# One hybrid decoder layer on one core: a kept block of zeros, a transposing swish, reordered FFN rounds and a paired last quarter

## The chip, the cores and the metric

The kernel runs on one core of a Trainium2 chip. Such a core has a matrix engine (TensorE, PE in the profile), a vector engine (VectorE, DVE), an activation engine (ScalarE, ACT), a general engine (GpSimd, POOL), an engine that issues transfers (SyncE, SP), an on-chip memory of 128 partitions (SBUF) and an accumulator memory for the matrix engine's results (PSUM). Each engine takes its instructions in its own fixed order and waits on semaphores for the others. The metric is device microseconds per execution; lower is better.

## The reference

One layer on 1024 tokens of width 1024, in fp32. `rmsnorm` and `layernorm` are the usual ones, and the six rows of `mod` come from the vector `c`.

```python
h = rmsnorm(x, pre_mix_g) * (1.0 + sc1) + sh1
glu_in, qkv, gates = split(h @ w_in)
u = u_val * sigmoid(u_gate)                        # 512 channels
u = causal_depthwise_conv(u, conv_w, conv_b)       # 31 taps
u = silu(layernorm(u, conv_ln_g, conv_ln_b))
y_conv = u @ w_conv_out
o = stick_breaking_attention(q, k, v)              # 8 heads of 64, strictly causal
y_att = o @ w_att_out
merged = sigmoid(g_conv) * y_conv + sigmoid(g_att) * y_att
x = x + ga1 * rmsnorm(merged @ w_o, post_mix_g)
h = rmsnorm(x, pre_ffn_g) * (1.0 + sc2) + sh2
gate, up = split(h @ w_ffn_in)                     # d_ff = 2816
x = x + ga2 * rmsnorm((silu(gate) * up) @ w_ffn_out, post_ffn_g)
```

In the attention a query's weights come from `sigmoid(z)` and a running product over the keys before it, so a 128-token block above the diagonal is zero.

## The kernel before

**Tiling.** Activations lie with channels on the partitions and tokens along the free axis, in two halves of 512 tokens. A product of fp32 matrices is made of three: each operand is split into a rounded part (`_hi`, made by ACT as a copy) and a remainder (`_lo`, made by VectorE as a subtraction), and PE multiplies hi·hi, lo·hi and hi·lo into one PSUM bank. A "product" below means 12 matmuls of 128 x 512, four row blocks by three.

**Stages**, with their place in the profiled execution: start, norm and `mod` (to 60 us); four head pairs of attention beside the GLU, the convolution and the projections of q, k, v (60 to 436); gate projections (436 to 591), the last of them beside the LayerNorm of the convolution; the two branch projections (574 to 669); `w_o` and the second norm (669 to 760); FFN input rounds (760 to 1190); FFN output and the closing norm (1190 to 1419).

**Order.** A scheduler sets each engine's order from the program and its own idea of durations. In some stretches the order is that in which the code is written: `pin(begin)` chains everything since `begin` on each engine. `load` issues a transfer from SP's queue, `store` from POOL's.

**Attention** (`head`, L522). Scores `z` of a query block become probabilities `be` on ACT and VectorE (a scan). PE transposes them in 128 x 128 blocks into a PSUM tile `tr` (L571), ACT copies that to `ahi` (L574), VectorE forms `alo` (L575), and PE multiplies both with the values into `av` (L580, L581). On a diagonal pair of blocks one of the four 128-column blocks is zero; it is transposed from a tile `zeros` in SBUF like any other.

**Early gate products** (the loop over GPAIRS before `sV.close()`). The gate projection is done by Strassen-like recombination: for each of six pairs, the product with B11 (bank `k1`) and with B21 (bank `k2`) are made early, and the other five products (`ka`, `kc`, L415) later. The B11 product goes as `e[0]` to DRAM; VectorE adds it to the B21 product (L628), ACT takes the sigmoid, and that goes to DRAM too. Both staging tiles have two buffers.

**LayerNorm and swish** (`ln_all`, L724). Two PE products of ones (`lnm`, `lnv` L748) give mean and variance. After scaling, for each of four channel tiles ACT writes `csig` (L756, sigmoid) and rewrites `cr` (L757, scale and bias), and VectorE multiplies them into `csil` (L760). The convolution holds its tokens in another order (eight phases of 128); the multiplication writes them back in token order, so it writes with a stride of eight elements. From `csil` the operands `chi` and `clo` (L721) of the branch projection are made.

**FFN rounds** (`ffn`, L1319). A round also combines five products: T2 (`ka`), T1 (`kc`), T3 (`ka` again, accumulating), B22 (`kc`) and T4 (`ka`), after two early ones from the `ke` stage (L1066). Its left operands are sums of weights (`s1`, `s2`, `s3`, `s4`) split by `w_op` into hi and lo (`s1o` and so on; `a22o` for T4); its right ones (`T_jo`, `B_jo`) are built once, j from 0 to 3, from the normalized activations. After T2 and T1 VectorE "takes" the bank (L1358: it adds the early product and writes SBUF), after T3 and B22 it adds the bank (L1373, L1376). `ffn` is a generator; the pinned code drives rounds 0 and 1 with `next(r0)` and `next(r1)` between the pieces of the right operands. The bank `ka` is reused for T3 only after T2 has been taken, and `kc` for B22 only after T1 has.

**Tail** (`finish`, L1613). For the last 256 columns PE sums squares (`fsum`, L1708), `rstd_from` makes the normalizer `frs` (ACT L151, L152, VectorE L153 to L155), and VectorE scales eight tiles (L1626, L1629) and adds the residual to each (L1529); four transfers write the output.

## Time and profile before

| | |
|---|---|
| timed runs | 1422.94, 1416.66, 1416.08 us (median 1416.66) |
| profiled execution | 1420.87 us, span 1419.1 us |
| PE busy | 1389.1 us (98%), 6886 instructions |
| VectorE, ACT, POOL busy | 1061.3 (75%), 650.8 (46%), 96.3 us (7%) |
| granted TensorE clock, mean | 0.99 |

The page gives, for one profiled execution, the busy time of each engine and the groups of instructions that cost most. A group's row has the source line, the engine, the operation, the tiles (output, then inputs) and the number of instructions with their durations. A row of the timeline has the start, the length and, in brackets, the idle time of the engine ahead of it with what ended that. A row of the waits has the waiting engine and line, what it waited for, the time in total, the number of waits and the longest. Neighbouring PE rows overlap, since matmuls are pipelined: the distance of their starts is the cost of one, not its duration.

### The profile page before, as it was taken

To read this page: it belongs to the slowest core of one execution; us is meant where nothing else is said; L and a number is where in the kernel's file an instruction comes from. 1 tells how busy PE (TensorE), PEld (TensorE's weight loads), DVE (VectorE), ACT (ScalarE), POOL (GpSimd) and SP (SyncE) were. 2 spreads that over 40 slices of the span, in tenths; PEclk is the share of its full clock that TensorE was granted. 3 is DMA by queue.
4 is the path that set the end of the run, shared out by engine and by line. 5 is a ranking of instruction groups with operands and counts; after the bars stand their busy time and mean duration, and the time that the engine had idled before them with its cause. 6 is when DMAs were issued, how large, how long until landed. Compare 5 with 4: busy or idle time off the path is not lost.

```text
span 1419.1 us, 18807 instructions
## 1 busy us (share of the span) xinstructions
PE 1389.1 (98%) x6886; PEld 1161.1 (82%) x6886; DVE 1061.3 (75%) x1602; ACT 650.8 (46%) x1136; POOL 96.3 (7%) x183
## 2 busy tenths in 40 slices
PE   7999999999999999999999999999999999999996
PEld 4888898898888878888877778888888887888886
DVE  6788688666776779779589878788777776785357
ACT  5275466354553547413356543334444444433441
POOL 0000000000000101000011110001111110000000
PEclk8899999999999999999999999999999999999999
DMA  9112032122163654784934535456777769588733
GB/s 383 64 45 75 30 110 84 45 80 99 51 204 104 224 178 165 282 280 133 375 121 163 180 146 171 165 177 206 252 254 252 261 235 390 178 331 287 279 117 119
DMA packets 91116, 258.73 MB, mean 182 GB/s; under 512 B 9744, under 2 KB 20112, under 8 KB 90000
## 3 DMA queue, kind: packets, MB, share of 16 engines
q1 hardware_dynamic: 75088, 202.99, 42.0%
q0 software_dynamic: 15936, 54.54, 10.2%
q8 instruction: 54, 0.88, 0.3%
q14 instruction: 38, 0.31, 0.1%
HBM read 190.91 MB, written 66.58 MB: 181 GB/s over the span
## 4 chain that ended last, share of the span: by engine, by line
PE 87%; DVE 6%; DMA 3%; ACT 2%; issue 1%; SPq 0%; DVEq 0%; ACTq 0%; POOLq 0%
PE ka L958 12%; PE ka L1489 9%; PE kc L958 7%; PE pwo L881 6%; PE pb L1489 4%; PE pgv L180 3%; PE pg L180 3%; PE pyc L180 3%; PE pya L180 3%; PE pv L481 3%; PE pcv L461 3%; PE ka L415 2%; PE tr L571 2%; PE ke L1066 2%; PE pq L180 2%; PE pgg L180 2%
## 5 line engine op out<-in xcount | busy, mean ns | idle before, releaser
L559 DVE TENSOR_TENSOR_SCAN ka<-ka 128x128 f32<-128x128 f32 (+2 forms) x96 | 91.4, 968 | 22.8 <-ACT ka L555 22.5
L555 ACT ACTIVATE ka<-z 128x128 f32<-128x128 f32 (+2 forms) x96 | 47.1, 496 | 59.1 <-PE z L554 32.6
L575 DVE TENSOR_TENSOR alo<-tr,ahi 128x512 fp32r<-128x512 f32 x80 | 53.2, 685 | 18.2 <-ACT ahi L574 17.7
L574 ACT ACTIVATE ahi<-tr 128x512 fp32r<-128x512 f32 x80 | 46.4, 602 | 37.7 <-PE tr L571 25.9
L1489 PE MATMUL ka<-gt,w2f 128*128 128x512 f32 x264 | 63.4, 389 | 0.1
L561 DVE TENSOR_TENSOR be<-be,ka 128x127 f32<-128x127 f32 (+2 forms) x96 | 53.4, 572 | 9.7 <-ACT be L556 5.0
L1489 PEld LDWEIGHTS ka<-gt,w2f 128*128 128x128 f32 x264 | 49.5, 188 | 10.8 <-issue 0.5
L1066 PE MATMUL ke<-b,w_hi 128*128 128x512 f32 x176 | 55.1, 394 | 0.0
L135 DVE SCALAR_TENSOR_TENSOR ada<-ada,cb 128x1024 f32<-128x1024 f32 x32 | 38.8, 1223 | 19.6 <-DMA ada<-in_ada_dram 19.6
L556 ACT ACTIVATE be<-z 128x128 f32<-128x128 f32 (+2 forms) x96 | 46.2, 496 | 9.6 <-PE tr L571 9.5
L571 PE MATMUL tr<-ident,be 128*128 128x128 f32 x288 | 47.8, 273 | 0.4 <-DVE alo L575 0.4
L580 PE MATMUL av<-ahi,vst 128*128 128x256 f32 x160 | 44.2, 292 | 0.0
L461 PE MATMUL pcv<-ph,cvw 128*128 128x128 f32 x320 | 42.5, 276 | 0.9 <-DMA ph<-v_d 0.9
L581 PE MATMUL av<-alo,vst 128*128 128x256 f32 x160 | 42.8, 293 | 0.0
L461 PEld LDWEIGHTS pcv<-ph,cvw 128*128 128x128 f32 x320 | 39.5, 192 | 1.6 <-issue 1.3
L1066 PEld LDWEIGHTS ke<-b,w_hi 128*128 128x128 f32 x176 | 33.0, 188 | 7.8 <-issue 1.0
L481 PE MATMUL pv<-wv_hi,hhi 128*128 128x256 f32 x128 | 36.8, 288 | 2.1 <-DVE qst L505 1.4
L159 ACT ACTIVATE gt<-X 128x512 fp32r<-128x512 f32 x33 | 20.4, 630 | 39.1 <-PE ka L1489 12.1
L481 PE MATMUL pv<-wv_hi,hlo 128*128 128x256 f32 x128 | 36.7, 287 | 0.0
L481 PE MATMUL pv<-wv_lo,hhi 128*128 128x256 f32 x128 | 36.4, 285 | 0.0
L551 PE MATMUL z<-kst,qst 128*128 128x256 f32 (+2 forms) x96 | 36.2, 382 | 0.0
L571 PEld LDWEIGHTS tr<-ident,be 128*128 128x128 f32 x288 | 34.7, 140 | 1.8 <-PE z L554 0.5
(532 smaller groups left out, 4108.5 us busy)
## 6 DMA issues: line engine op xcount, KB each, us to landing
w_d<-w2o POOLq DMA_DIRECT2D x44, 512.0 KB, 8.1
...
w2r<-in_w_dram SPq DMA_DIRECT2D x44, 256.0 KB, 4.0
...
```

Source lines behind the costliest of these rows:

```text
L180: pe.matmul(bank, st[:, cols], mv[k][:, c * CH:(c + 1) * CH], start=(i == 0 and s == 0), stop=(i == n - 1 and s == 2))
L461: pe.matmul(cv[:, gi * TM:(gi + 1) * TM], wts[n][:, at:at + P], ph[:, g, SH - 1 - d:SH - 1 - d + TM], start=(d == 0), stop=(d == SH - 1))
L481: pe.matmul(pv[:, :256], st[k][:, tcols], mv[:, wc], start=(k == 0 and i == 0), stop=(k == KT - 1 and i == 2))
L555: act.activation(kap[:, s_lo:s_hi], z[:, zo:zo + w], AF.Sigmoid, bias=0.0, scale=-0.125)
L559: dve.tensor_tensor_scan(rev, rev, rev, init, op0=ALU.mult, op1=ALU.bypass)
L561: dve.tensor_tensor(beta[:, :m], beta[:, :m], kap[:, s_lo + 1:s_lo + 1 + m], op=ALU.mult)
L571: pe.transpose(tr[:, o:o + P], src, ident)
L575: dve.tensor_tensor(alo, tr, ahi, op=ALU.subtract)
L881: pe.matmul(bank_, st[:, cols], mv[k][:, cs], start=(k == 0 and q == 0), stop=(k == KT - 1 and q == 2))
L958: pe.matmul(bank_, st[:, cols], t[:, mv], start=(first and j == 0 and s == 0), stop=(j == HK - 1 and s == 2), skip_group_check=not first)
L1066: pe.matmul(kbs[f], wes[f][st][:, cols], t[:, mv], start=(i == 0 and j == 0 and q == 0), stop=(j == HK - 1 and q == 2), skip_group_check=i ...
L1489: pe.matmul(dst, w[st][:, cols], g[mv], start=first and s == 0, stop=last and s == 2, skip_group_check=more)
```

## The change

Five edits, independent of each other in the code.

1. **Kept zero block.** Two pairs of tiles (`ahid`, `alod`) get their first 128 columns set to zero once, before the attention. A diagonal pair of blocks uses one of them in turn: the zero block is put first, only the other three are transposed, and only columns 128 to 511 are copied and subtracted.
2. **Early gate products in twos.** Two pairs share a step. Both B11 products are made and staged, then each B21 product accumulates onto its B11 product in the same bank, and ACT takes the sigmoid from there. The VectorE adds are gone.
3. **Swish in token order.** Both ACT passes write with the stride of eight elements into `csig` and `csil`, and VectorE multiplies in place without a stride.
4. **FFN rounds reordered.** In round 0 the T4 product and its addition stand ahead of the multiplication and store of `w_`. Round 1's raw weights and its first operand (`s1`, `s2`, `s2o`) come before B22's low parts in the pinned order, and round 1's next steps are woven with round 0's last.
5. **Paired last quarter.** In the last `finish`, operations span both halves of a pair (`128 x 2 x 256`). ACT copies three residual pairs into PSUM ahead of time; POOL does pair 0, VectorE pairs 2, 3 and 1.

```diff
@@ -521,0 +522,8 @@
+            diag_t = []
+            for i in range(2):
+                t = [pa.tile([P, CH], F32R, name=f"{nm}d{i}") for nm in ("ahi", "alo")]
+                for x in t:
+                    dve.tensor_copy(x[:, :P], zeros)
+                diag_t.append(t)
+            ndiag = count()
+
@@ -564,0 +573 @@
+                            on = jp == c
@@ -567,0 +577,2 @@
+                                    if on and jj == 1 and ii == 0:
+                                        continue
@@ -569,7 +580,11 @@
-                                    src = zeros if (jp == c and jj == 1 and ii == 0) else probs[ii][:, jo:jo + P]
-                                    o = jj * 256 + ii * P
-                                    pe.transpose(tr[:, o:o + P], src, ident)
-                            ahi = pa.tile([P, CH], F32R, tag="ahi", name=f"ahi{tag}_{c}_{jp}", bufs=2)
-                            alo = pa.tile([P, CH], F32R, tag="alo", name=f"alo{tag}_{c}_{jp}", bufs=2)
-                            act.activation(ahi, tr, AF.Copy)
-                            dve.tensor_tensor(alo, tr, ahi, op=ALU.subtract)
+                                    o = (jj ^ on) * 256 + ii * P
+                                    pe.transpose(tr[:, o:o + P], probs[ii][:, jo:jo + P], ident)
+                            if on:
+                                ahi, alo = diag_t[next(ndiag) % 2]
+                                used = slice(P, CH)
+                            else:
+                                ahi = pa.tile([P, CH], F32R, tag="ahi", name=f"ahi{tag}_{c}_{jp}", bufs=2)
+                                alo = pa.tile([P, CH], F32R, tag="alo", name=f"alo{tag}_{c}_{jp}", bufs=2)
+                                used = slice(0, CH)
+                            act.activation(ahi[:, used], tr[:, used], AF.Copy)
+                            dve.tensor_tensor(alo[:, used], tr[:, used], ahi[:, used], op=ALU.subtract)
@@ -579 +594 @@
-                                cols = slice(jj * 256, jj * 256 + 256)
+                                cols = slice((jj ^ on) * 256, (jj ^ on) * 256 + 256)
@@ -618,13 +633,17 @@
-            for i in GPAIRS:
-                raw = wp.tile([P, T], F32, tag="wraw", name=f"ew{i}")
-                load(raw, win[20 + 2 * i])
-                e = [sgp.tile([P, CH], F32, tag="sg", name=f"ee{q}_{i}", bufs=2) for q in range(2)]
-                k1 = bank(f"k1_{i}")
-                prod0(k1, w_op(f"a11_{i}", raw[:, :CH], act, dve), "B11")
-                act.activation(e[0], k1, AF.Copy)
-                store(e_d0[i], e[0])
-                k2 = bank(f"k2_{i}")
-                prod0(k2, w_op(f"a12_{i}", raw[:, CH:], act, dve), "B21")
-                dve.tensor_tensor(e[1], k2, e[0], op=ALU.add)
-                act.activation(e[1], e[1], AF.Sigmoid, bias=0.0, scale=1.0)
-                store(s_d[2 * i][:, :CH], e[1])
+            for i0 in range(0, len(GPAIRS), 2):
+                two = GPAIRS[i0:i0 + 2]
+                ek, a12 = {}, {}
+                for i in two:
+                    raw = wp.tile([P, T], F32, tag="wraw", name=f"ew{i}")
+                    load(raw, win[20 + 2 * i])
+                    ek[i] = bank(f"k1_{i}")
+                    prod0(ek[i], w_op(f"a11_{i}", raw[:, :CH], act, dve), "B11")
+                    a12[i] = w_op(f"a12_{i}", raw[:, CH:], act, dve)
+                    e0 = sgp.tile([P, CH], F32, tag="sg", name=f"ee0_{i}", bufs=2)
+                    act.activation(e0, ek[i], AF.Copy)
+                    store(e_d0[i], e0)
+                for i in two:
+                    prod0(ek[i], a12[i], "B21", False)
+                    e1 = sgp.tile([P, CH], F32, tag="sg", name=f"ee1_{i}", bufs=2)
+                    act.activation(e1, ek[i], AF.Sigmoid, bias=0.0, scale=1.0)
+                    store(s_d[2 * i][:, :CH], e1)
@@ -756,2 +774,0 @@
-                act.activation(sg, a, AF.Sigmoid, bias=b_, scale=g)
-                act.activation(a, a, AF.Identity, bias=b_, scale=g)
@@ -759,3 +776,4 @@
-                ar, sr = (t.rearrange("p (r m) -> p r m", r=PH) for t in (a, sg))
-                (pool if ct in SILU_POOL else dve).tensor_tensor(
-                    o.rearrange("p (m r) -> p r m", r=PH), ar, sr, op=ALU.mult)
+                ar = a.rearrange("p (r m) -> p r m", r=PH)
+                act.activation(sg.rearrange("p (m r) -> p r m", r=PH), ar, AF.Sigmoid, bias=b_, scale=g)
+                act.activation(o.rearrange("p (m r) -> p r m", r=PH), ar, AF.Identity, bias=b_, scale=g)
+                dve.tensor_tensor(o, o, sg, op=ALU.mult)
@@ -1378,0 +1397,5 @@
+            if f == 0:
+                yield
+                prod(ka, a22o, "T4", False)
+                dve.tensor_tensor(p1, ka, p1, op=ALU.add)
+                yield
@@ -1382 +1405,2 @@
-            prod(ka, a22o, "T4", False)
+            if f:
+                prod(ka, a22o, "T4", False)
@@ -1384 +1408,2 @@
-                dve.tensor_tensor(p1, ka, p1, op=ALU.add)
+                if f:
+                    dve.tensor_tensor(p1, ka, p1, op=ALU.add)
@@ -1428,0 +1454,3 @@
+        raw_w(1)
+        next(r1)
+        next(r0)
@@ -1436,0 +1465,2 @@
+        next(r1)
+        next(r0)
@@ -1438 +1467,0 @@
-        raw_w(1)
@@ -1618,0 +1648,5 @@
+            if last:
+                xp = {}
+                for mm_ in (2, 3, 1):
+                    xp[mm_] = bank(f"x1p{mm_}").rearrange("p (a b) -> p a b", a=2)
+                    act.activation(xp[mm_], xrs[c, mm_][:, :, cols], AF.Copy)
@@ -1619,0 +1654,22 @@
+            if last:
+                r2 = rs.unsqueeze(1).to_broadcast([P, 2, n])
+                y0, y1, y2_, y3 = (ytile[yy[m // 2], m % 2][:, :, cols] for m in range(4))
+
+                def put(m, y):
+                    load(out[2 * m:2 * m + 2, :, dcols].rearrange("n p t -> p n t"), y)
+
+                begin = len(nc.cur_bb.bb.instructions)
+                pool.tensor_tensor(y0, y0, r2, op=ALU.mult)
+                pool.tensor_tensor(y0, y0, xrs[c, 0][:, :, cols], op=ALU.add)
+                for m, y in ((2, y2_), (3, y3)):
+                    for i in range(2):
+                        dve.scalar_tensor_tensor(y[:, i], last[2 * (m - 2) + i][:, cols],
+                                                 gpost2[:, 2 * m + i:2 * m + i + 1], rs, op0=ALU.mult, op1=ALU.mult)
+                    add(dve, y, y, xp[m])
+                    put(m, y)
+                dve.tensor_tensor(y1, y1, r2, op=ALU.mult)
+                add(dve, y1, y1, xp[1])
+                put(0, y0)
+                put(1, y1)
+                pin(begin)
+                return
```

Three places where instructions move. First, ACT beside the last gate operands (`s2o_5`, `s1o_5` and so on are hi parts for pair 5; `gw`, `gv`, `gc` are sigmoids of gates). Before:

```order
L756 ACTIVATE csig0_4939<-cr0_4869,vec_133 128x1024
L159 ACTIVATE a22_4_5357<-gw4b_5169 128x512
L757 ACTIVATE cr0_4869<-cr0_4869,vec_133 128x1024
L159 ACTIVATE s1o_5_5403<-gs1_5_5375 128x512
L756 ACTIVATE csig1_4944<-cr1_4871,vec_133 128x1024
L686 ACTIVATE gv_3_5176<-gv_3_5176 128x512
L159 ACTIVATE s2o_5_5383<-gs2_5_5376 128x512
L757 ACTIVATE cr1_4871<-cr1_4871,vec_133 128x1024
L159 ACTIVATE s3o_5_5419<-gs3_5_5377 128x512
L756 ACTIVATE csig2_4949<-cr2_4873,vec_133 128x1024
```

With the change:

```order
L777 ACTIVATE csig0_4839<-cr0_4769,vec_133 128x8x128
L778 ACTIVATE csil0_4840<-cr0_4769,vec_133 128x8x128
L777 ACTIVATE csig1_4844<-cr1_4771,vec_133 128x8x128
L159 ACTIVATE s4o_4_5239<-gs2_4_5178 128x512
L778 ACTIVATE csil1_4845<-cr1_4771,vec_133 128x8x128
L777 ACTIVATE csig2_4849<-cr2_4773,vec_133 128x8x128
L159 ACTIVATE s2o_5_5283<-gs2_5_5276 128x512
L778 ACTIVATE csil2_4850<-cr2_4773,vec_133 128x8x128
L777 ACTIVATE csig3_4854<-cr3_4775,vec_133 128x8x128
L705 ACTIVATE gw_3_5077<-gw_3_5077 128x512
L159 ACTIVATE s1o_5_5303<-gs1_5_5275 128x512
L778 ACTIVATE csil3_4855<-cr3_4775,vec_133 128x8x128
```

Before, passes of the swish alternate with the gates' operations, and `s1o_5` stands behind two passes; now seven of the eight passes stand ahead of `s1o_5`.

Second, VectorE in the FFN's rounds 0 and 1 (`s1_1` is `s1` of round 1, `uw_0` holds the taken banks of round 0). Before:

```order
L1358 TENSOR_TENSOR uw_0_7441<-ka_0_7356,p1_0_7440 128x512
L1365 TENSOR_TENSOR s0_0_7112<-w1_0_7325,s0_0_7112 128x512
L949 TENSOR_TENSOR s4o_0_7457<-s0_0_7112,s4o_0_7457 128x512
L1048 SCALAR_TENSOR_TENSOR B22_0o_7432<-y1_0_6700,mod_156,B22_0o_7432 128x512
L1048 SCALAR_TENSOR_TENSOR B22_1o_7434<-y1_1_6551,mod_156,B22_1o_7434 128x512
L1048 SCALAR_TENSOR_TENSOR B22_2o_7436<-y1_2_6602,mod_156,B22_2o_7436 128x512
L1048 SCALAR_TENSOR_TENSOR B22_3o_7438<-y1_3_6653,mod_156,B22_3o_7438 128x512
L1358 TENSOR_TENSOR uw_0_7441<-kc_0_7357,p1_0_7440 128x512
L1096 SCALAR_TENSOR_TENSOR y0_2_6290<-y0_2_6290,mod_156,t2_2_7199 128x512
L1096 SCALAR_TENSOR_TENSOR y0_3_6332<-y0_3_6332,mod_156,t2_3_7227 128x512
L1080 TENSOR_TENSOR T4_2o_7478<-y0_2_6290,T4_2o_7478 128x512
L1080 TENSOR_TENSOR T4_3o_7481<-y0_3_6332,T4_3o_7481 128x512
```

With the change:

```order
L1359 TENSOR_TENSOR s1_1_7346<-w1u1_7342 128x512
L1360 TENSOR_TENSOR s2_1_7347<-s1_1_7346,w1g1_7340 128x512
L967 TENSOR_TENSOR s2o_1_7351<-s2_1_7347,s2o_1_7351 128x512
L1376 TENSOR_TENSOR uw_0_7355<-ka_0_7256,p1_0_7354 128x512
L1383 TENSOR_TENSOR s0_0_7012<-w1_0_7225,s0_0_7012 128x512
L967 TENSOR_TENSOR s4o_0_7371<-s0_0_7012,s4o_0_7371 128x512
L1376 TENSOR_TENSOR uw_0_7355<-kc_0_7257,p1_0_7354 128x512
L1066 SCALAR_TENSOR_TENSOR B22_0o_7332<-y1_0_6600,mod_156,B22_0o_7332 128x512
L1066 SCALAR_TENSOR_TENSOR B22_1o_7334<-y1_1_6451,mod_156,B22_1o_7334 128x512
L1066 SCALAR_TENSOR_TENSOR B22_2o_7336<-y1_2_6502,mod_156,B22_2o_7336 128x512
L1066 SCALAR_TENSOR_TENSOR B22_3o_7338<-y1_3_6553,mod_156,B22_3o_7338 128x512
```

Three operations of round 1 came ahead of the take of T2, the take of T1 came ahead of B22's low parts, and the low parts of T4's third and fourth blocks came behind the addition of T3.

Third, VectorE behind the normalizer of the last 256 columns. Before:

```order
L1626 TENSOR_TENSOR yc11_0_11976<-yc11_0_11976,frs01_12178 128x256 x2
L1626 TENSOR_TENSOR yc11_1_11977<-yc11_1_11977,frs01_12178 128x256 x2
L1629 SCALAR_TENSOR_TENSOR yc21_0_11984<-ka_0_10335,gpost2_160,frs01_12178 128x256
L1629 SCALAR_TENSOR_TENSOR yc21_0_11984<-ka_1_10336,gpost2_160,frs01_12178 128x256
L1629 SCALAR_TENSOR_TENSOR yc21_1_11985<-ka_2_10337,gpost2_160,frs01_12178 128x256
L1629 SCALAR_TENSOR_TENSOR yc21_1_11985<-ka_3_10338,gpost2_160,frs01_12178 128x256
L1529 TENSOR_TENSOR yc11_0_11976<-yc11_0_11976,xr0_0_11964 128x256 x2
L1529 TENSOR_TENSOR yc11_1_11977<-yc11_1_11977,xr0_1_11967 128x256 x2
L1529 TENSOR_TENSOR yc21_0_11984<-yc21_0_11984,xr0_2_11970 128x256 x2
L1529 TENSOR_TENSOR yc21_1_11985<-yc21_1_11985,xr0_3_11973 128x256 x2
```

With the change:

```order
L1666 SCALAR_TENSOR_TENSOR yc21_0_11884<-ka_0_10235,gpost2_160,frs01_12078 128x256
L1666 SCALAR_TENSOR_TENSOR yc21_0_11884<-ka_1_10236,gpost2_160,frs01_12078 128x256
L1558 TENSOR_TENSOR yc21_0_11884<-yc21_0_11884,x1p2_12081 128x2x256
L1666 SCALAR_TENSOR_TENSOR yc21_1_11885<-ka_2_10237,gpost2_160,frs01_12078 128x256
L1666 SCALAR_TENSOR_TENSOR yc21_1_11885<-ka_3_10238,gpost2_160,frs01_12078 128x256
L1558 TENSOR_TENSOR yc21_1_11885<-yc21_1_11885,x1p3_12083 128x2x256
L1670 TENSOR_TENSOR yc11_1_11877<-yc11_1_11877,frs01_12078 128x2x256
L1558 TENSOR_TENSOR yc11_1_11877<-yc11_1_11877,x1p1_12085 128x2x256
```

Sixteen operations became eight; POOL's queue ends with two of its own (L1662, L1663). In SP's queue the transfers follow in the order of pairs 2, 0, 3 and 1.

## The prediction

> **What bounds the kernel now.** I read the page's first part, then a table of stretches of the span, then the waits of TensorE alone, since an engine that is never free makes every other engine's idle time worthless.
>
> ```profile
> PE 1389.1 (98%) x6886; PEld 1161.1 (82%) x6886; DVE 1061.3 (75%) x1602; ACT 650.8 (46%) x1136; POOL 96.3 (7%) x183
> 150.00:300.00 150.00, 150.00 (x943) 132.27 (x942) 103.99 (x150) 76.04 (x158) 5.65 (x3) 1.00 0.19 62
> 500.00:550.00 50.00, 48.53 (x204) 37.80 (x203) 45.42 (x75) 27.41 (x43) 4.85 (x9) 1.00 0.45 154
> 760.00:900.00 140.00, 135.98 (x581) 108.18 (x580) 113.61 (x172) 66.25 (x107) 20.46 (x38) 1.00 0.52 176
> 1405.00:1419.00 14.00, 2.85 (x18) 2.28 (x16) 6.96 (x19) 1.22 (x3) 0.00 (x0) 0.76 0.27 92
> ```
>
> In a stretch's row stand its length, then the busy time of PE, PEld, DVE, ACT and POOL, the granted clock, and the DMA share. PE is busy 98% of the span, all of it between 150 and 300. So the time falls only where PE gets fewer instructions, where PE now waits, or in the last 14 us, where PE has 2.85 us of work and the end hangs on VectorE. What PE waits for:
>
> ```profile
> PE ka L958 <- DVE uw L1373: 1.4, 2, 0.9
> PE ka L415 <- DVE gv L703: 1.2, 1, 1.2
> PE kc L958 <- DVE s1o L949: 0.8, 1, 0.8
> PE kc L958 <- DVE uw L1358: 0.7, 1, 0.7
> PE ka L415 <- ACT s2o L159: 0.3, 1, 0.3
> PE ka L958 <- DVE uw L1358: 0.2, 1, 0.2
> PE kc L415 <- DVE s1o L402: 0.2, 1, 0.2
> ```
>
> The change touches the two places named here: the gates (L415, 1.7 us in three waits) and the first FFN rounds (L958). Its other parts touch attention, the swish and the tail.
>
> **Kept zero block: −3.5 us.** The attention stage loses its transposes of zeros.
>
> ```profile
> L571 PE MATMUL tr<-ident,zeros x32: 270/272/279, 89.2 to 422.1; 128*128 128x128 f32 x32
> 150.61 0.93 PE L571 MATMUL tr<-ident,be 128*128 128x128 f32 x7
> 71.53 1.23 DVE L169 TENSOR_TENSOR wv_lo<-wv_raw,wv_hi 128x1024 fp32r<-128x1024 f32 x1 [10.21 <-PE pk L331]
> ```
>
> The 272 ns are latency. Seven in a row take 0.93, so one more costs (0.93−0.27)/6 = 0.11 us of PE, and 32 of them 3.5 us. PE is full there, so all of it counts. The copies of a diagonal block shrink to 384 columns. The four new casts on VectorE come ahead of `wv_lo`, in 10.21 us of idle time; without that cover they would cost about 4 × 0.3. Bounds −2.5 (a product catches up with its copies) and −4.0.
>
> **Early gate products in twos: −1.0 us.** PE's products stay as many. Six VectorE adds (L628) go, and ACT's sigmoid reads PSUM. The two products of a pair are now separated by the other pair's, and the first halves are done earlier, so the convolution's result, which queues behind them, is loaded earlier.
>
> ```profile
> L628 DVE TENSOR_TENSOR ee<-k,ee x6: 685/691/692, 469.4 to 505.9; 128x512 f32<-128x512 f32 x6
> e_d<-ee POOLq DMA_DIRECT2D x6, 256.0 KB, 4.1
> s_d<-ee POOLq DMA_DIRECT2D x6, 256.0 KB, 3.8
> ```
>
> VectorE is busy 45.42 of 50 us in that stretch and ends the 1.2-us wait at L703; 4.1 us of adds less should remove it. All three L415 waits gone are −1.7. The new danger is that a staging tile (two buffers) waits for its store, 4 us, with ACT in order behind it and so the sigmoids and casts of the other gates. Between two uses of a buffer PE has two products of 12 matmuls, 5.4 us; a store that takes 3 us longer than the median would cost +1.5. I take −1.0, bounds −1.7 and +1.5.
>
> **Swish in token order: +5.1 us, the term that decides.** The strided write moves from VectorE's product to ACT's two passes.
>
> ```profile
> L756 ACT ACTIVATE csig<-cr,vec x4: 1231/1240/1250, 553.6 to 565.5; 128x1024 f32<-128x1024 f32 x4
> L757 ACT ACTIVATE cr<-cr,vec x4: 1227/1230/1232, 555.5 to 567.2; 128x1024 f32<-128x1024 f32 x4
> L760 DVE TENSOR_TENSOR csil<-cr,csig x4: 2181/2186/2200, 558.3 to 569.7; 128x1024 f32<-128x1024 f32 x4
> L721 DVE TENSOR_TENSOR clo<-csil,chi x4: 1216/1243/1250, 572.3 to 585.1; 128x1024 fp32r<-128x1024 f32 x4
> L574 ACT ACTIVATE ahi<-tr x80: 580/598/646, 89.8 to 429.0; 128x512 fp32r<-128x512 f32 x80
> L575 DVE TENSOR_TENSOR alo<-tr,ahi x80: 664/684/693, 91.9 to 429.6; 128x512 fp32r<-128x512 f32 x80
> ```
>
> VectorE's strided write of 1024 columns takes 2.186, a contiguous operation of that size 1.22 to 1.24: the stride costs it 0.95 us, and 4 × 0.95 = 3.8 us go from VectorE, which does not set the time here. No row shows ACT writing with a stride. Call its duration S. Its lower bound is 1.235 (free); the nearest row says that a stride costs one more pass over the elements. On equal tiles ACT takes 598 where VectorE takes 684, so I scale 0.95 × 598/684 = 0.83 and take S = 2.1, an estimate. The upper bound is two more passes, S about 3.0.
>
> ACT is in order, so S counts in the queue. In the changed order seven of the eight passes stand ahead of `s1o_5`, the last gate's operand, and four short operations (0.52 apart, as the rows at 558.93 and 559.45 are).
>
> ```profile
> 545.29 1.02 PE L748 MATMUL lnv<-la,ones 128*128 128x512 f32 x2
> 553.59 1.25 ACT L756 ACTIVATE csig<-cr,vec 128x1024 f32<-128x1024 f32 x1
> 558.93 0.61 ACT L686 ACTIVATE gv<-gv 128x512 f32<-128x512 f32 x1
> 559.45 0.62 ACT L159 ACTIVATE s2o<-gs 128x512 fp32r<-128x512 f32 x1
> 561.04 2.60 PE L415 MATMUL kc<-T1o,s1o 128*128 128x512 f32 x10 [0.20 <-DVE s1o L402]
> ```
>
> From the LayerNorm's variance product (in the group at 545.29, the second one queued about 0.4 later) to the first `csig` go 7.9 us. So `s1o_5` is ready 7.9 + 7S + 4 × 0.52 = 7S + 10.0 after it. PE has seven products of twelve between the two; the row at 561.04 gives 2.60 for ten with its latency, 0.227 per matmul, thus 84 × 0.227 + 0.6 for restarts = 19.7. PE stalls for 7S − 9.7: nothing at S = 1.235 (a slack of 1.0), 5.0 at 2.1 (half of it already one product earlier, at `s2o_5`), 11.3 at 3.0. With the restart I count 5.1. Behind it, one more pass and ten short operations (9 us) feed the convolution's projection; PE has 46 matmuls, 10.4 us, which just cover them.
>
> [...] The new writes are 32 bytes apart. [...]
>
> **FFN rounds reordered: −2.0 us.** PE's products keep their order; VectorE's and ACT's change.
>
> ```profile
> 828.65 0.69 DVE L1358 TENSOR_TENSOR uw<-ka,p 128x512 f32<-128x512 f32 x1 [0.59 <-PE ka L958]
> 833.90 0.68 DVE L1358 TENSOR_TENSOR uw<-kc,p 128x512 f32<-128x512 f32 x1
> 834.73 0.93 PE L958 MATMUL kc<-B_0o,s4o 128*128 128x512 f32 x3 [0.68 <-DVE uw L1358]
> 837.82 0.68 DVE L1373 TENSOR_TENSOR uw<-ka,uw 128x512 f32<-128x512 f32 x1
> 838.65 0.94 PE L958 MATMUL ka<-T_0o,a 128*128 128x512 f32 x3 [0.93 <-DVE uw L1373]
> 845.66 0.50 PE L958 MATMUL kc<-T_0o,s1o 128*128 128x512 f32 x1 [0.83 <-DVE s1o L949]
> 848.43 0.93 PE L958 MATMUL ka<-T_0o,s3o 128*128 128x512 f32 x3 [0.21 <-DVE uw L1358]
> ```
>
> VectorE's steps are 0.61 apart (0.66 for B). I walk the new order from T3's low parts, which end at 828.0. Round 1's `s1`, `s2` and the low part of `s2o` come first, to 830.6; the take of T2 to 831.3 (T3, due at 831.17, is 0.2 late); `s4o` to 833.2; the take of T1 to 833.9, before B22's low parts and no longer after them. So B22 starts at 834.2 in place of 834.73. `a` and the sum of T3 end at 837.8, and T4 starts there and not at 838.65. Now T4's third and fourth low parts are late instead, at 840.45, and T4 ends at 840.75 against 841.49. Round 1's T2 and T1 follow without a wait, since `s1o` is ready at 840.4, and its T3 starts at 840.75 + 8 × 0.68 = 846.2, with the take of its T2 at 844.9. Against 848.43 this is −2.2; I take −2.0. Bounds −2.7 (all waits) and −0.3 (each low part one step later than walked).
>
> **Paired last quarter: −1.5 us.**
>
> ```profile
> 1409.84 1.43 DVE L1626 TENSOR_TENSOR yc<-yc,frs 128x256 f32<-128x256 f32 x4
> 1411.19 1.65 DVE L1629 SCALAR_TENSOR_TENSOR yc<-ka,gpost,frs 128x256 f32<-128x256 f32 x4
> 1412.76 2.76 DVE L1529 TENSOR_TENSOR yc<-yc,xr 128x256 f32<-128x256 f32 x8
> L169 POOL TENSOR_TENSOR wv_lo<-wv_raw,wv_hi 128x1024 fp32r<-128x1024 f32 x2 | 5.5, 2761 | 47.0 <-ACT wv_hi L159 47.0
> ```
>
> Sixteen VectorE operations fill 1409.84 to 1415.5. One of the four output pairs goes to POOL: 2.76 us for 1024 columns make 1.4 for 512, two of them 2.8, ending at about 1412.8. VectorE keeps four scalings (0.39 apart) and four paired operations of 512 columns (0.6): 1.6 + 2.4 = 4.0, ending at 1413.9 in place of 1415.5, before the same output transfer. The copies of the residual into PSUM are ACT's, idle then. Bounds: −1.7, and 0 if POOL takes twice as long, since two transfers stand behind POOL's in SP's queue.
>
> **The sum.** −3.5 − 1.0 + 5.1 − 2.0 − 1.5 = −2.9 against the profiled execution's 1420.87 (span 1419.1). That execution is 4.2 above the median of the three timed runs, 1416.66, and the sum does not depend on it: 1416.66 − 2.9 = **1413.8**.
>
> **The rivals.**
> - **ACT's strided write is free** (S = 1.235, slack kept). Then −8.0: 1408.7. For it: ACT's rows show other rates than VectorE's. Against it: L760's 2.186, and the 32-byte step is the same.
> - **The waits only move**: the gates and the FFN rounds give nothing, since the next late operand takes the place of the first (as T4's low parts do above), and ACT pays. −3.5 − 1.5 + 5.1 = +0.1: 1416.8.
> - **Slower: ACT pays two more passes** (S = 3.0). The stall is 11.3, with everything else as forecast −8.0 + 11.4 = +3.4: 1420.1. It decides from 7S − 9.7 > 8.0, S above 2.5; beyond 0.5% only from S = 3.5, or with a gate store that holds ACT as well.
>
> **How the numbers follow.** Chances: forecast 0.50, free write 0.36, waits only move 0.08, slower 0.06. About 0.5% of 1416.66, 7.1 us, is what a measurement can tell from no change. Faster by more than that means below 1409.6: two thirds of the free-write case (0.24) and the forecast's low edge with S near 1.6 (0.04) give 0.28. Slower beyond 1423.7 needs the last case at its worst, or two bounds at once: 0.05. The rest, 0.67, lies within. The range runs from the free write with the other terms somewhat better, 1407.0, to the third case with a little loss, 1418.5; the forecast's own is 1411 to 1417.
>
> **What would show it.** No transposes from `zeros`, and 3.5 us less PE work. The swish rows on ACT at about 2.1 us (1.24: the free write; 3.0: the slower case) and a PE wait of 5 us at `s2o_5` and `s1o_5` near 555 to 575. No wait at L703's successor, and none of ACT on the stores of `ee`. T4 of round 0 some 0.8 us earlier relative to T1 of round 0. A last output transfer issued about 4.1 us after the normalizer is done, against 5.7. An ACT row under 1.5 with no saving, or a PE wait in a place not named here, would make the prediction wrong in its reasons.

## The result, and the profile after

The changed kernel takes 1423.43 us (median of 16 runs, 1419.43 to 1429.93) against 1417.04 for the kernel before (16 runs, 1414.75 to 1422.94). The ratio is 1.0038, with a 95% interval from 1.0026 to 1.0050: slower by 0.4%. That is less than the 0.5% that the prediction took for no change, but 10 us above the forecast of 1413.8 and 5 us above the end of the range.

The first part of the page and two rows of the table of stretches (length, then busy PE, PEld, DVE, ACT, POOL, granted clock, DMA share) of the changed kernel:

```profile
PE 1383.2 (98%) x6854; PEld 1154.6 (81%) x6854; DVE 1049.1 (74%) x1592; ACT 657.2 (46%) x1139; POOL 98.2 (7%) x185
550.00:600.00 50.00, 47.05 (x197) 37.92 (x198) 32.61 (x43) 29.91 (x32) 4.86 (x9) 0.97 0.65 236
600.00:760.00 160.00, 156.69 (x686) 128.46 (x686) 121.94 (x178) 59.14 (x80) 4.32 (x8) 1.00 0.61 209
```

The same two rows of the kernel before:

```profile
550.00:600.00 50.00, 49.80 (x219) 40.58 (x218) 42.10 (x53) 29.01 (x36) 5.40 (x10) 1.00 0.71 245
600.00:760.00 160.00, 159.94 (x703) 131.42 (x702) 124.66 (x181) 61.38 (x83) 4.32 (x8) 1.00 0.61 216
```

PE has its 32 instructions less, yet it stands idle for 3 us in each of two stretches that were full. The granted clock of the first one fell to 0.97. The waits of PE in the changed kernel (total, number, longest):

```profile
PE pwo L899 <- DVE sga L839: 3.3, 1, 3.3
PE ka L415 <- ACT s2o L159: 2.3, 1, 2.3
PE pcv L461 <- DMA ph<-v_d: 1.6, 1, 1.6
...
```

The second row is the swish, as forecast. The first, at the beginning of `w_o`, was named nowhere in the prediction.

To place the time, I took from each trace the start of the first matmul of six kinds and the distances between them. Left out is the start of the program, which no part of the change touches: the first V projection comes at 70.01 us in the profile after and at 74.33 in the profile before. The profile after is also the shortest of its 16 executions (1419.43 us). The profile of e1 below, of the same kernel, lies near the median (1424.19), and its rows are 4.1 us longer in sum. In us:

| from, to | before | after | e1, the same kernel | e1 − before |
|---|---|---|---|---|
| first V projection, first early gate product (attention) | 387.16 | 385.12 | 385.23 | −1.9 |
| first early gate product, first attention projection (gates, swish, convolution's projection) | 164.26 | 168.27 | 169.84 | +5.6 |
| first attention projection, first `w_o` product | 43.52 | 46.94 | 48.43 | +4.9 |
| first `w_o` product, first `ke` product | 89.14 | 89.23 | 90.87 | +1.7 |
| first `ke` product, last matmul (FFN) | 649.06 | 647.09 | 646.38 | −2.7 |
| last matmul, end | 11.61 | 11.00 | 11.01 | −0.6 |
| sum | 1344.75 | 1347.65 | 1351.76 | +7.0 |

Attention, swish, FFN and end moved in the forecast's direction. The two rows in the middle, +6.6 us together, are what the prediction has no term for. They also vary between two executions of one kernel: the wait at `w_o` is 3.26 us in the profile after and 4.75 in e1.

### The profile page after: what moved, and what is told of

The parts are those of the page before. It is cut to its first block, busy times and chain, and to the rows that moved or that the text cites. A ratio compares the mean times of both kernels' runs of the same rounds, so it can differ in the third digit from the quotient of the medians.

```text
span 1417.7 us, 18697 instructions
## 1 busy us (share of the span) xinstructions
PE 1383.2 (98%) x6854; PEld 1154.6 (81%) x6854; DVE 1049.1 (74%) x1592; ACT 657.2 (46%) x1139; POOL 98.2 (7%) x185
## 4 chain that ended last, share of the span: by engine, by line
PE 63%; issue 18%; DVE 9%; DMA 5%; ACT 3%; POOL 2%; POOLq 0%; SPq 0%; DVEq 0%; ACTq 0%
PE ka L1518 9%; PE pwo L899 6%; PE ka L976 6%; PE pb L1518 4%; PE pgv L180 3%; PE pg L180 3%; PE kc L976 3%; PE pv L481 3%; PE pgg L180 2%; PE pk L180 2%; PE pcv L461 2%; PE k L415 2%; PE pa L1518 2%; PE tr L581 2%; PE pq L180 2%
## 5 line engine op out<-in xcount | busy, mean ns | idle before, releaser
L519 DVE TENSOR_TENSOR klo<-pk,kst 64x512 fp32r<-64x512 f32 x32 | 22.0, 689 | 22.8 <-ACT kst L516 22.4
L590 DVE TENSOR_TENSOR alo<-tr,ahi 128x512 fp32r<-128x512 f32 x48 | 32.2, 684 | 7.7 <-ACT ahi L589 7.4
L899 PE MATMUL pwo<-mhi,wo_hi 128*128 128x512 f32 x88 | 34.6, 395 | 3.3 <-DVE sga L839 3.3
L589 ACT ACTIVATE ahi<-tr 128x512 fp32r<-128x512 f32 x48 | 28.1, 602 | 17.4 <-PE tr L581 12.0
```

Of the source, the lines that this page charges most:

```text
L899: pe.matmul(bank_, st[:, cols], mv[k][:, cs], start=(k == 0 and q == 0), stop=(k == KT - 1 and q == 2))
```

## The experiments

Every kernel here computes the whole layer. Ratios are against the kernel before in the same set of runs, with 95% intervals; 0.001 is 1.4 us. A difference of two ratios is uncertain by 2.4 to 3 us, unless another figure is given. "Edit 1" to "edit 5" are the parts as the change numbers them.

### First set: which part costs what

**e1**: the changed kernel once more, without an edit.

> The changed kernel once more, for a second profile and its time beside the others. Theory A (the swish stalls PE): the waits of PE at s2o and s1o of the last gate pair (2.3 and 0.4 us in the first profile) and the slow product behind them (4.75 us for twelve matmuls in place of 2.88) stand in this profile too, and the execution is 4 to 8 us longer than the kernel before. Rival B (the profiled execution was faster than the median by 4 us because its waits are smaller than in others): here these waits, or the one at the first product of w_o (3.3 us), are clearly longer.

Measured 1.0046 [1.0032, 1.0059]. Both theories hold in part: the waits of the first profile stand here too, and two of them are clearly longer, 2.01 us in place of 0.44 at `s1o` and 4.75 in place of 3.26 at `w_o`.

**e2**: the changed kernel with the old swish.

```diff
-                ar = a.rearrange("p (r m) -> p r m", r=PH)
-                act.activation(sg.rearrange("p (m r) -> p r m", r=PH), ar, AF.Sigmoid, bias=b_, scale=g)
-                act.activation(o.rearrange("p (m r) -> p r m", r=PH), ar, AF.Identity, bias=b_, scale=g)
-                dve.tensor_tensor(o, o, sg, op=ALU.mult)
+                act.activation(sg, a, AF.Sigmoid, bias=b_, scale=g)
+                act.activation(a, a, AF.Identity, bias=b_, scale=g)
+                ar, sr = (t.rearrange("p (r m) -> p r m", r=PH) for t in (a, sg))
+                (pool if ct in SILU_POOL else dve).tensor_tensor(
+                    o.rearrange("p (m r) -> p r m", r=PH), ar, sr, op=ALU.mult)
```

> All of the change but the swish, which is as before. Theory A: the waits at s2o and s1o and the slow product go, so 7 us less than the whole change and about 1 us less than before; the wait at the first product of w_o (3.3 us) stays or grows, since PE now comes there earlier and VectorE frees its bank no sooner. Rival C (another part than the swish costs the time): within 2 us of the whole change.

Measured 1.0013 [0.9999, 1.0027]. Without its most expensive part the change should have been 8 us faster than the kernel before; it is not faster at all. So the greater part of the miss lies elsewhere than in the swish.

**e3**: the kernel before with the new swish alone (the same lines, the other way round).

> The kernel before with the swish of the change alone. Theory A: ACT's passes at 2.2 to 2.4 us and a PE wait of 2 to 6 us before the last gate products, 4 to 8 us slower than before. Rival C: ACT's passes as long, but within 1.5 us of the kernel before, because its schedule puts other work between.

Measured 1.0062 [1.0050, 1.0075], +8.8 us. The passes, here in the changed kernel (shortest, median and longest in ns, then the first and last start):

```profile
L777 ACT ACTIVATE csig<-cr,vec x4: 2195/2272/2427, 543.8 to 557.5; 128x1024 f32<-128x1024 f32 x4
L778 ACT ACTIVATE csil<-cr,vec x4: 2294/2334/2372, 546.0 to 560.6; 128x1024 f32<-128x1024 f32 x4
L779 DVE TENSOR_TENSOR csil<-csil,csig x4: 1226/1226/1226, 548.3 to 563.0; 128x1024 f32<-128x1024 f32 x4
```

ACT pays 2.27 and 2.33 us where it paid 1.24 and 1.23, and VectorE 1.226 in place of 2.186. The stall in e3 stands at the operand that the prediction named:

```profile
PE kc L415 <- ACT s1o L159: 5.3, 1, 5.3
...
PE pyc L180 <- ACT wc_hi L159: 1.0, 1, 1.0
```

Of the 8.8 us, 5.3 are this wait and 1.0 a second one at the first projection of the convolution, which the kernel before does not have. About 2 more follow from the rate behind the first: PE's next matmuls, some ten of them, are 0.427 us apart and not 0.227. The changed kernel shows it after its own wait, in a row of its timeline:

```profile
555.53 4.75 PE L415 MATMUL ka<-T2o,s2o 128*128 128x512 f32 x12 [2.31 <-ACT s2o L159]
560.72 0.73 PE L415 MATMUL kc<-T1o,s1o 128*128 128x512 f32 x2 [0.44 <-ACT s1o L159]
```

Twelve matmuls take 4.75 us; at 0.227 they would take 2.9 (11 × 0.227 + 0.4).

**e4**: the changed kernel with the old early gate products.

```diff
-            for i0 in range(0, len(GPAIRS), 2):
-                two = GPAIRS[i0:i0 + 2]
...
+            for i in GPAIRS:
...
+                prod0(k2, w_op(f"a12_{i}", raw[:, CH:], act, dve), "B21")
+                dve.tensor_tensor(e[1], k2, e[0], op=ALU.add)
```

> All of the change but the early gate products in twos. If the gates bring the 1.0 us that was forecast: 1 us more than the whole change. If the earlier gates are what lets PE run into ACT's passes and into the wait at w_o (rival D): 2 to 5 us less than the whole change.

Measured 1.0070 [1.0054, 1.0087]: without the pairs the change is 3.4 us slower still, uncertain by 3.0. So beside the strided swish the gates in twos help, and rival D is refuted; whether they help by more than the 1.0 us forecast, the intervals do not tell.

### Second set: where the 8 us of e2 are

**f1**: the changed kernel without the kept zero block.

```diff
-            diag_t = []
...
-            ndiag = count()
...
-                                    if on and jj == 1 and ii == 0:
-                                        continue
+                                    src = zeros if (jp == c and jj == 1 and ii == 0) else probs[ii][:, jo:jo + P]
```

> All of the change but the kept zero block. Theory E: the kept zero block shifts the ring of PSUM banks by one, so that the first product of w_o gets the bank of the last product of the attention projection (with the zero block bank 0 was last used by its tile 7_1, without it by 5_1), and PE waits 4.8 us there and then runs some 2 us at half rate. Without the zero block that wait is gone and the 1.8 us that it saves in the attention come back: 4.9 us less than the whole change. Rival F (PE comes to w_o earlier than VectorE can follow, whatever the bank): the wait of 3 us or more stays, and the time is 1 to 2 us above the whole change.

Measured 1.0009 [0.9997, 1.0021]. The part that was forecast to save 3.5 us costs 5.2: without it the whole is that much faster than e1. From the first attention projection to the first `w_o` product go 43.52 us again, as before the change, so the wait is gone.

**f2**: the kernel before with the kept zero block alone.

> The kernel before with the kept zero block alone. Theory E: 1.8 us less in the attention, 4.5 us of wait and 2 us of half rate at the first product of w_o, so 4 to 5 us slower than before. Rival F: the wait is that of PE's lead, under 2 us, and the kernel is 0 to 2 us faster than before.

Measured 1.0029 [1.0017, 1.0041], +4.1 us. Two of its waits:

```profile
PE pwo L896 <- DVE sga L836: 3.1, 1, 3.1
...
PE pcv L461 <- DMA ph<-v_d: 1.5, 1, 1.5
```

The first appears with the zero block alone, some 250 us behind the last diagonal block (416.3 to 666.7 in f2). It has to do with banks. In the built programs the first product of `w_o` is given PSUM bank 0 with and without the zero block. Without the zero block bank 0 held the product of the sixth attention projection before; with it, that of the eighth and last. The ring of three banks from which these products are drawn is entered one place on. Why the scheduler turns it there I did not trace. What it means shows in the timelines. VectorE, at the end of the attention projections in the kernel before:

```profile
670.70 1.23 DVE L721 TENSOR_TENSOR mlo<-yc,mhi 128x1024 fp32r<-128x1024 f32 x1 [1.13 <-ACT mhi L159]
671.84 1.28 DVE L821 TENSOR_TENSOR sga<-pya,sga 128x512 f32<-128x512 f32 x2
```

And PE there:

```profile
668.82 0.62 PE L180 MATMUL pya<-ohi,wa_lo 128*128 128x512 f32 x2
669.27 0.39 PE L881 MATMUL pwo<-mhi,wo_hi 128*128 128x512 f32 x1
669.50 0.39 PE L881 MATMUL pwo<-mlo,wo_hi 128*128 128x512 f32 x1
```

VectorE empties the last two `pya` banks from 671.84 to 673.12, while PE has been in `w_o` since 669.27: VectorE is 3.9 us behind PE there, and nobody minds. In the changed kernel PE's next bank is one of these two (timeline of e1, VectorE):

```profile
672.71 1.28 DVE L839 TENSOR_TENSOR sga<-pya,sga 128x512 f32<-128x512 f32 x2
```

and of PE:

```profile
674.13 0.76 PE L899 MATMUL pwo<-mhi,wo_hi 128*128 128x512 f32 x1 [4.75 <-DVE sga L839]
674.69 0.63 PE L899 MATMUL pwo<-mlo,wo_hi 128*128 128x512 f32 x1
675.12 0.63 PE L899 MATMUL pwo<-mhi,wo_lo 128*128 128x512 f32 x1
...
677.87 0.40 PE L899 MATMUL pwo<-mhi,wo_hi 128*128 128x512 f32 x1
678.11 0.39 PE L899 MATMUL pwo<-mlo,wo_hi 128*128 128x512 f32 x1
```

VectorE's last evacuation ends at 673.99, and PE starts at 674.13. It has waited 4.75 us, and the distance of its matmuls is 0.43 us until 677.6 and 0.24 from then on.

**f3**: the kernel before with edits 2, 4 and 5, so without zero block and swish.

```diff
-            for i in GPAIRS:
+            for i0 in range(0, len(GPAIRS), 2):
...
+            if f == 0:
+                yield
+                prod(ka, a22o, "T4", False)
...
+                pool.tensor_tensor(y0, y0, r2, op=ALU.mult)
```

> Gates in twos, FFN rounds and tail of the change; zero block and swish as before. Theory E with the terms read from the traces (FFN -2.0, tail -0.7, gates 0 to -1): 2.7 to 3.7 us faster than before, with no wait at the first product of w_o. Rival F: that wait appears here too, 1 to 3 us.

Measured 1.0004 [0.9992, 1.0015]. A saving of about 3 us was expected and none came, so one of these three parts takes back what the others give (see h3 and h4).

**f4**: the changed kernel with the old swish and with one bank taken, by a write that nobody reads, ahead of the first `w_o` product, which thereby gets another bank, last used by the LayerNorm.

```diff
         load(cb2, cb_d)
+        dve.memset(dbank("skip0")[:, :1], 0.0)
         for n in range(KT):
             yb = dbank(f"pwo0_{n}")
```

> Zero block, gates, FFN rounds and tail of the change, swish as before, and one unused bank taken ahead of the first product of w_o (one VectorE memset of a column), which gives that product bank 7, free since the LayerNorm. Theory E: no wait at the first product of w_o, and the zero block's 1.8 us stay: 1.8 us faster than the kernel with gates, FFN and tail alone, 6 to 7 us faster than the same without the moved bank. Rival F: a wait of 3 us or more remains at w_o.

Measured 0.9986 [0.9973, 0.9998]; e2, the same kernel without the added line, had 1.0013. The first attention projection to the first `w_o` product takes 43.52 us, as before; 48.18 in e2. The wait is gone. From the first V projection to the end the two profiles differ by 6.7 us, within the 6 to 7 expected; the two ratios, from different sets, by only 3.8.

### Third set: the bank, the half rate and the stride

**g1**: the whole change with the bank moved.

```diff
+        dve.memset(dbank("skip0")[:, :1], 0.0)
```

> The whole change, with one unused bank taken ahead of the first product of w_o, so that this product gets bank 7 and not that of the last attention projection. Theory E: the wait of 3.3 to 4.8 us there goes with the half rate behind it (2 us), the swish stalls stay: 5 to 6.5 us less than the whole change, 0 to 2 us above the kernel before. Rival F (VectorE sets the start of w_o whatever the bank): less than 2 us.

Measured 0.9989 [0.9975, 1.0003]. PE passes from one stage to the next without a pause:

```profile
668.41 0.61 PE L180 MATMUL pya<-ohi,wa_lo 128*128 128x512 f32 x2
668.87 0.39 PE L899 MATMUL pwo<-mhi,wo_hi 128*128 128x512 f32 x1
669.09 0.39 PE L899 MATMUL pwo<-mlo,wo_hi 128*128 128x512 f32 x1
```

Against e1 the one line gives 8.1 us (0.0057), more than the 5 to 6.5 expected. The two profiles account for 6.0 of them (43.52 in place of 48.43, and 89.73 in place of 90.87); the two ratios come from different sets, and their difference is uncertain by about 2.7 us.

**g2**: the kernel before with edits 1, 4 and 5 and the bank moved: the old gates and the old swish.

```diff
-            for i0 in range(0, len(GPAIRS), 2):
+            for i in GPAIRS:
...
-                dve.tensor_tensor(o, o, sg, op=ALU.mult)
+                (pool if ct in SILU_POOL else dve).tensor_tensor(
...
+        dve.memset(dbank("skip0")[:, :1], 0.0)
```

> Zero block, FFN rounds and tail of the change with the moved bank; gates and swish as before. Sum of the traces: -1.9 - 2.0 - 0.7 = -4.6, less up to 1 us where PE waits for VectorE at w_o: 3.6 to 4.6 us faster than before, and 1.5 to 2.5 faster than the same with the gates in twos, if those bring nothing without the strided swish. If the gates bring the 1.0 us forecast, 1 us slower than it.

Measured 0.9957 [0.9943, 0.9971], 1412.90 us: faster than both kernels, and the best of all runs. It is 4.1 us faster than f4, which differs by the gates in twos alone: without the strided swish these cost time.

**g3**: the kernel before with a swish in which ACT reads with a stride and writes without one. The stride is another than in e3. Each read is 128 elements (512 bytes) from the one before, since the eight phases lie 128 columns apart; the write in e3 steps by eight elements (32 bytes). The expectation below says eight elements for the read, which is not what the kernel does.

```diff
-                act.activation(sg, a, AF.Sigmoid, bias=b_, scale=g)
-                act.activation(a, a, AF.Identity, bias=b_, scale=g)
+                ar = a.rearrange("p (r m) -> p m r", r=PH)
+                act.activation(sg.rearrange("p (m r) -> p m r", r=PH), ar, AF.Sigmoid, bias=b_, scale=g)
+                act.activation(o.rearrange("p (m r) -> p m r", r=PH), ar, AF.Identity, bias=b_, scale=g)
+                dve.tensor_tensor(o, o, sg, op=ALU.mult)
```

> The kernel before with the swish in token order, where ACT reads with the stride of eight elements and writes without one. If only the strided write costs a second pass: ACT's passes at 1.25 us, no stall at s1o, the time of before within 1 us. If a strided read costs the same: passes at 2.2 to 2.4 us and 8 to 9 us slower, like the kernel with the strided write alone.

Measured 1.0053 [1.0032, 1.0074], no better than e3:

```profile
L758 ACT ACTIVATE csig<-cr,vec x4: 2181/2255/2294, 550.7 to 565.4; 128x1024 f32<-128x1024 f32 x4
L759 ACT ACTIVATE csil<-cr,vec x4: 2114/2231/2257, 552.9 to 568.6; 128x1024 f32<-128x1024 f32 x4
```

A stride costs ACT about one more microsecond per pass of 1024 columns here, whether it is one of 32 bytes on the side that is written (2.27 and 2.33 us in the changed kernel, 1.24 and 1.23 before) or one of 512 bytes on the side that is read (2.26 and 2.23). A read with a step of 32 bytes was not run.

**g4**: e2 with 19 matmuls that nobody needs, between the last attention projection and the first `w_o` product. PE is busy while it waits for the bank; the bank is not moved.

```diff
+        warm = psg.tile([P, CH], F32, tag="ln", name="warm", bufs=1)
+        with tc.issue_after(last_mm.ins):
+            for q in range(19):
+                pe.matmul(warm, mhi[0][:, :P], mhi[0][:, :CH], start=(q == 0), stop=(q == 18))
+            dve.memset(warm[:, :1], 0.0)
```

> The kernel without the swish (zero block, gates, FFN, tail; the bank as the zero block leaves it), with 19 more matmuls of 128 x 512 into an unused bank between the last attention projection and the first product of w_o, 4.3 us of PE work where PE waits 4.5 us. Theory G (the half rate after a long wait comes from PE's idleness): the first w_o matmuls are 0.227 apart from the start, and the kernel is 2.4 us faster than without the added matmuls, though PE does more. Rival H (the half rate comes from elsewhere, for example the load of transfers): matmuls 0.427 apart remain, and the time is the same.

Measured 0.9994 [0.9980, 1.0008], against 1.0013 for e2.

```profile
663.24 4.47 PE L849 MATMUL warm<-mhi 128*128 128x512 f32 x19
667.62 0.47 PE L906 MATMUL pwo<-mhi,wo_hi 128*128 128x512 f32 x1
667.93 0.39 PE L906 MATMUL pwo<-mlo,wo_hi 128*128 128x512 f32 x1
668.16 0.40 PE L906 MATMUL pwo<-mhi,wo_lo 128*128 128x512 f32 x1
```

The stage is as late as in e2 (47.90 us behind the first attention projection, e2 48.18), but its matmuls are 0.23 apart from the second on. From the first `w_o` product to the first `ke` product go 89.26 us; in e2 91.87. So the low rate comes from PE's idleness, not from the data or the bank, and costs 2.6 us there (the last section shows which idleness brings it). The time agrees with that (−2.7), though the two intervals overlap.

### Fourth set: the terms one by one

What was still open: whether moving the bank helps by itself, and which of edits 2, 4 and 5 took the gain in f3.

**h1**: the kernel before with the bank moved.

```diff
+        dve.memset(dbank("skip0")[:, :1], 0.0)
```

> The kernel before with nothing but the unused bank taken ahead of the first product of w_o. Theory E (the moved bank helps only where it removes the wait): the same as before within 1 us. Rival K (the moved bank has a gain of its own, by another order of banks in w_o and the FFN): 2 us or more faster.

Measured 0.9996 [0.9985, 1.0008]. Where nothing waited there, the line does nothing.

**h2**: edit 1 with the bank moved.

```diff
+            diag_t = []
...
+        dve.memset(dbank("skip0")[:, :1], 0.0)
```

> Kept zero block alone, with the bank moved. Traces: 1.9 us faster than before. Forecast: 3.5. If neither: the zero block is worth nothing on the chip once its transposes are gone.

Measured 0.9985 [0.9972, 0.9998]: −2.1 us. With f2 (+4.1) it says that the same edit costs or saves by the bank that follows from it. The attention stage is 2.2 us shorter (385.00), not 3.5. Here the profiles agree: with the zero block the stage takes 385.0 to 385.5 us in ten of them, without it 387.0 to 387.3 in the other ten. Of the missing 1.3 us, 0.6 are in f2's second row: PE is sooner at the convolution, whose data come by a transfer, and waits 1.5 us for it in place of 0.9. The rest was not traced.

**h3**: the kernel before with edit 2 alone.

```diff
-                dve.tensor_tensor(e[1], k2, e[0], op=ALU.add)
+                    prod0(ek[i], a12[i], "B21", False)
```

> Gates in twos alone. Forecast: 1.0 us faster than before; traces of the mixed kernels: 0 to 1 us slower, since PE then waits for the hi part of the projection weight (1.1 us at the first pyc product) and at w_o.

Measured 1.0032 [1.0018, 1.0046]: +4.5 us. Its waits:

```profile
PE pwo L885 <- ACT mhi L159: 2.1, 1, 2.1
...
PE kc L415 <- DVE s1o L402: 1.4, 2, 0.9
...
PE pyc L180 <- ACT wc_hi L159: 1.1, 1, 1.1
...
PE ka L415 <- DVE gw L711: 0.9, 1, 0.9
```

The waits of 1.2 us at `gv` and 0.3 at `s2o` are gone, and the operands behind them are late instead. The stretch from the early gates to the attention projection became 2.1 us longer. Then the whole chain of ACT and VectorE behind it comes later against PE, until PE stops for `mhi` inside `w_o`, and half rate follows a little later (h3, PE):

```profile
675.37 0.73 PE L885 MATMUL pwo<-mhi,wo_hi 128*128 128x512 f32 x2 [2.07 <-ACT mhi L159]
...
676.75 0.66 PE L885 MATMUL pwo<-mlo,wo_hi 128*128 128x512 f32 x1
677.22 0.63 PE L885 MATMUL pwo<-mhi,wo_lo 128*128 128x512 f32 x1
```

From `w_o` to `ke` go 93.16 us in place of 89.14.

**h4**: the kernel before with edits 4 and 5.

```diff
+            if f == 0:
+                yield
+                prod(ka, a22o, "T4", False)
...
+                pool.tensor_tensor(y0, y0, r2, op=ALU.mult)
```

> FFN rounds and tail alone. Forecast: 3.5 us faster than before; traces: 2.0 and 0.7, so 2.7 faster.

Measured 0.9976 [0.9964, 0.9989]: −3.4 us, against −2.0 − 1.5 in the forecast. So f3's missing gain is the gates' (f3 − h4 = +4.0 us).

### Fifth set: the stores under the gates in twos

In h3 ACT shows the danger that the prediction named, a staging tile that waits for its store. The two staging tiles share two buffers. The waits of ACT from 470 to 600 us, first in h3, then in the kernel before:

```profile
ACT ee L628 <- DMA s_d<-ee: 11.2, 2, 6.1
...
ACT ee L629 <- DVE ee L628: 13.3, 4, 6.2
```

Behind the two waits in h3 stand casts of the late operands. But ACT waits no less in the kernel before, there for VectorE's adds, so the waits alone prove nothing. Whether they make the 4.5 us was tried by taking them away: three buffers of its own for the sigmoid's staging tile, five in all.

**i1**: h3 with the additional buffers. **i2**: f3 with them.

```diff
-                    e1 = sgp.tile([P, CH], F32, tag="sg", name=f"ee1_{i}", bufs=2)
+                    e1 = pc.tile([P, CH], F32, tag="sge1", name=f"ee1_{i}", bufs=3)
```

> The gates in twos alone (3 buffers of their own for the sigmoid's staging tile, so 5 in place of 2 for the two staging tiles), beside 1.0032 with two buffers. In that run ACT waited 5.1 and 6.1 us for stores of the sigmoid to free a staging tile, with the casts of the late operands queued behind. Store theory: these two ACT waits go, the first early gate product comes to the first attention projection in 164 to 165 us in place of 166.3, no wait for mhi of 2 us at w_o, and the time is 0.998 to 1.000. Rival (the late operands are late for VectorE's and ACT's own order, whatever the stores do): ACT's waits move to VectorE or PE, and the time stays at 1.002 to 1.004.

> The same with the reordered FFN rounds and the paired last quarter. With two buffers it was 1.0004, the FFN rounds and the tail without the gates 0.9976. Store theory: 0.996 to 0.9975, the gates cost nothing any more. Rival: 1.000 as before.

Measured 1.0255 [1.0238, 1.0272] and 1.0258 [1.0236, 1.0279]: 36 us slower, which neither theory expected. The waits for the stores are gone from ACT. But the scheduler, no longer held back by the buffers, put all twelve early products on end and the operands of the others behind them. The first casts of `T2o` start at 439.4 us in h3, at 493.6 here. PE in i1:

```profile
PE ka L415 <- ACT T2o L159: 13.1, 3, 7.6
```

and a row of its table of stretches:

```profile
500.00:560.00 60.00, 41.05 (x140) 29.64 (x141) 56.04 (x88) 27.85 (x44) 2.16 (x4) 0.78 0.29 92
```

PE stands idle for 19 of 60 us there, at a granted clock of 0.78. So the two runs do not tell whether the stores cost the 4.5 us, since they changed the order as well; they show that the two shared staging buffers are also what spreads the early products over the stage. No run has the additional buffers beside the zero block.

## Why the prediction was wrong, point by point

The forecast was a gain of 2.9 us, and 5.4 were lost (6.5 in e1). The step that failed is the first term, which took the kept zero block for a change of its own stage alone. The measured terms, by ratios, where a part was run alone:

| part | forecast | measured |
|---|---|---|
| kept zero block itself | −3.5 | −2.1 (h2) |
| the bank that it turns | no term | +6.2 (f2 − h2) |
| early gate products in twos | −1.0 | +4.5 alone (h3), −3.4 beside the swish (e1 − e4) |
| swish in token order | +5.1 | +8.8 alone (e3), +4.7 in the whole (e1 − e2) |
| FFN rounds and tail | −3.5 | −3.4 (h4) |

The terms without the gates add up: zero block, swish, FFN and tail, run alone, make 4.1 + 8.8 − 3.4 = +9.5, and e4, which has them all, +9.9. The gates' term is the one that has no value of its own: +4.5 alone (h3), +4.0 beside FFN and tail (f3 − h4), +4.1 with the zero block as well (f4 − g2), and −3.4 beside the swish. It may be that they help where ACT and VectorE are late already; no run tests that.

With the bank moved the whole change comes to −1.6 us (g1, −3.5 to +0.4), an interval that holds the −2.9 of the forecast. So the bank makes up the miss of the sum within the uncertainty (e1 − g1 is 8.1 us). That the other terms fit so well is luck: swish and gates cost 8.8 and 4.5 us alone, where 5.1 and −1.0 were forecast, but 4.5 together (g1 − g2), where 4.1 were forecast.

1. **"Kept zero block: −3.5 us", bounds −2.5 and −4.0: this step failed.** It priced 32 transposes of 0.11 us and assumed that the edit stays in the stage in which it is written. The transposes went, and 2 us with them. But the edit also turned the ring of banks for a product 250 us later, and that put VectorE's lateness of 3.9 us, which was hidden, in front of PE. f2, h2, f4 and g1 with h1 as the control show it. Neither bound could hold it, since both were bounds of the price of a transpose.
2. **"Swish in token order: +5.1 us": right in mechanism and place.** S was 2.27 and 2.33, with 2.1 forecast and 1.235 (the "free write") the strongest rival, which is refuted. ACT pays for the stride here as VectorE did before (2.186 us against 1.24), in writing with steps of 32 bytes and, as g3 shows with 2.26 and 2.23 us, in reading with steps of 512 bytes; without a step its passes took 1.24 and 1.23. By 7S − 9.7 the stall would be 6.4 at S = 2.3; e3 has 5.3 in one, e1 2.3 + 2.0. What was mis-sized is "with the restart I count 5.1": it allowed 0.1 for the restart, and half rate costs about 2 us more. In e3 the next operand is 1.0 us late too, which the 46 matmuls "just cover" in the prediction.
3. **"Early gate products in twos: −1.0 us": wrong alone, and the rival "the waits only move" is right in kind.** That rival was given 0.08 and had the waits move at no loss. The step that failed is "all three L415 waits gone are −1.7": two went, and others came for them. The danger that the part named, ACT waiting for a store, did come (11.2 us of ACT in h3); that it is what makes PE late was not shown. The bounds, −1.7 and +1.5, did not hold the +4.5.
4. **"FFN rounds reordered: −2.0 us": right.** The profile after shows what was walked, T3 at 0.20 late, T4 late by its own small wait, and T3 of round 1 sooner (88.3 us after the first `ke` product, 90.0 before):

```profile
832.68 0.93 PE L976 MATMUL ka<-T_0o,s3o 128*128 128x512 f32 x3 [0.20 <-DVE uw L1376]
...
839.18 0.93 PE L976 MATMUL ka<-T_0o,a 128*128 128x512 f32 x3 [0.46 <-DVE uw L1391]
...
847.86 0.84 PE L976 MATMUL ka<-T_0o,s3o 128*128 128x512 f32 x3
```

   From the first `ke` product to the last matmul it is −2.0 in the profile after, −2.7 in e1, and −1.6 in h4.
5. **"Paired last quarter: −1.5 us": a size off.** The last matmul to the end gained 0.6 to 0.8 us (11.00 in the profile after, 10.78 in h4, against 11.61). VectorE's and POOL's operations came in the order that was walked. The profile after, VectorE:

```profile
1408.58 0.42 DVE L155 SCALAR_TENSOR_TENSOR frs<-frs01a,frs 128x256 f32<-128x256 f32 x1
...
1412.78 0.69 DVE L1558 TENSOR_TENSOR yc<-yc,x1p 128x512 f32<-128x512 f32 x1
```

   The last operation ends 4.47 us after the normalizer (1413.47 − 1409.00); before it was 5.72 (1415.52 − 1409.80), so 1.25 us came free, where 1.6 were forecast, and about half of it reached the end. What takes the rest behind the last transfer was not tried.
6. **The rivals.** "ACT pays two more passes" (S = 3.0) gave the measured sign for a cause that did not happen. What did happen was no rival: a new wait far from the edit. The last sentence of the prediction asked for it, "a PE wait in a place not named here".

Open remain two things. One is what makes the gates in twos late by themselves (the fifth set). The other is that f4 and g1 differ by the swish, 4.2 us by their profiles from the V projection on, but only 0.4 by their ratios, which come from two sets of runs and are uncertain by 2.7.
